# Gated FFN of a hybrid decoder step: up products by seven block products a pair, down products spread between the pairs

## The chip, the core and the metric

The kernel runs on one core of one Trainium2 chip. The metric is the time of one execution on the device in microseconds (us). TensorE is the matrix engine (PE in the profile, PEld its weight loads), VectorE is DVE, ScalarE is ACT, GpSimd is POOL, SyncE is SP. Lines L1 and so on are lines of the kernel's source.

## What is computed

One inference step of four trunk layers for 512 prompt tokens and 64 sample tokens together: 576 columns, kept as two halves of 288 (256 prompt, 32 sample). Layer 0 mixes by pools and a gated delta rule, layer 1 by a short convolution; behind each stands the channel mixer that this change is about:

```python
def conv_ffn(h, buf, w_up, conv_w, w_down):
    up = h @ w_up                                  # 1024 -> 2 * 2816
    gate, val = up[..., :D_FF], up[..., D_FF:]
    gc, new_buf = causal_dwconv(gate, buf, conv_w) # three taps
    return (jax.nn.silu(gc) * val) @ w_down, new_buf
...
        h = rmsnorm(x, norm_ffn[l])
        y, f_b = conv_ffn(h, ffn_buf[l], w_up[l], ffn_conv_w[l], w_down[l])
        x = x + y
```

The results have fp32 precision: each product is made of three, of a high part and a low part of both operands (high by high, high by low, low by high).

## The kernel before

Activations stand with features on the partitions: a row tile of 128 features by 576 tokens. A product takes a weight tile of 128 x 128 as the stationary operand and 288 token columns as the moving one; `gemm` (L216) issues, for each of the tiles of the inner dimension, six matmuls (three parts, two token halves).

Weights come as **units** of up to 1024 columns (`Feed`, L76). `load` queues a unit's transfer on SP into one of two `raw` buffers, `split` makes the two parts: ScalarE copies the high part `wh` (L111) and VectorE subtracts it for the low part `wl` (L113). `get` hands out the next unit and issues the work for those behind it. Each engine works off its instructions in the order in which they were issued; a semaphore wait on one holds up all behind it on that engine.

The channel mixer is `ffn`: the 22 tiles of hidden features go in two halves of 11. For each tile `f` (a **pair**: gate tile and value tile) come the gate product over eight k-tiles, the multiplication by the norm's factor of a token (`ext_mul`, L260 and L262), the convolution (L271, L273), silu (L1062), the value product, and the gated result `g`, split again into `gh`, `gl` (L279 to L285). After the 11 pairs of a half, eight **down products** with that half's 11 k-tiles follow, each added to its residual row tile `x` (L343). So there are 22 x 2 x 8 x 6 = 2112 matmuls for up and 8 x 22 x 6 = 1056 for down in each of the two channel mixers.

Before each channel mixer stands `out_proj`: eight products of 48 matmuls; after each, VectorE adds the residual, and `norm_operand` (L290, L291) makes high and low part of the scaled row tile, the operand of the next up products. The norm's own factor `rT` is worked out beside the first product (`norm_end`). The last down products of the second mixer and the final norm are in `last` (products at L1108, by halves of the tokens).

Of the kernel before, what the change touches and what calls it, by code (L numbers as in the profile page):

```python
# [74 lines left out]

class Feed:  # L76
    """Weights of the products in the order in which they are used: loaded ahead and split into two parts."""

    def __init__(self, tc, pool, units):
        self.tc, self.nc, self.pool, self.units = tc, tc.nc, pool, units  # L80
        self.raw, self.hl = {}, {}
        self.nd = self.ns = self.n = 0
        self.between = None
        self.slow = ()

    def cuts(self, i, w):
        """the first in halves, for an early start"""
        return ((0, 512), (512, w)) if i == 0 else ((0, w),)

    def load(self, upto):  # L90
        while self.nd < min(upto, len(self.units)):
            src, w = self.units[self.nd]
            t = self.pool.tile([128, 1024], F, tag="raw", name="raw", bufs=RAWB)
            for a, b in self.cuts(self.nd, w):
                self.nc.sync.dma_start(out=t[:, a:b], in_=src[:, a:b])
                if self.between and self.nd == 0 and a == 0:
                    self.between()
            self.raw[self.nd] = t
            self.nd += 1

    def split(self, upto):
        while self.ns < min(upto, len(self.units)):
            self.load(self.ns + 1)
            t = self.raw.pop(self.ns)
            w = self.units[self.ns][1]
            if self.ns < len(self.units) - 2:
                h, l = (self.pool.tile([128, 1024], R, tag=n, name=n, bufs=HLB) for n in ("wh", "wl"))
            else:
                h, l = (self.extra.tile([128, 768], R, tag=n, name=n, bufs=2) for n in ("eh", "el"))
            for a, b in self.cuts(self.ns, w):  # L110
                self.nc.scalar.activation(out=h[:, a:b], in_=t[:, a:b], func=AF.Copy)  # L111
                e = self.nc.gpsimd if self.ns in self.slow else self.nc.vector
                e.tensor_tensor(out=l[:, a:b], in0=t[:, a:b], in1=h[:, a:b].bitcast(F), op=SUB)  # L113
            self.hl[self.ns] = (h, l)
            self.ns += 1

    def get(self):
        i = self.n
        self.n += 1
        self.split(i + HLB)  # L120
        self.load(i + HLB + RAWB)
        return self.hl.pop(i)
# [10 lines left out]
LY = (4, 8)  # L133
# [8 lines left out]
RAWB, HLB, WB = 2, 2, 6  # L142


def body(ctx, tc, I, O):
# [9 lines left out]
    wk = pool(ctx, "wk")  # L155
    xm = pool(ctx, "xm")
    ps = pool(ctx, "ps", space=PSUM)

    cst = com.tile([128, NCST], F, name="cst")
    vec = com.tile([128, NVEC], F, name="vec")  # L160

    def C(name, rows=128):
        o, w = CST[name]
        return cst[0:rows, o:o + w]
# [9 lines left out]
    def W(name="w"):  # L174
        return wk.tile([128, 711], F, tag="w", name=name, bufs=WB)

    def bank(name="sm"):
        return ps.tile([128, 512], F, tag="sm", name=name, bufs=4)

    def acc2(name="mm"):  # L180
        return ps.tile([128, 2, 512], F, tag="mm", name=name, bufs=2)

    units = []
    for c in ORD.split():
        if c != "g":
            units.append((I["w_in_ab"][{"p": 0, "q": 4, "k": 8, "v": 12, "z": 16}[c[0]] + int(c[1])], 1024))
    for m in range(8):
        units.append((I["w_out_ab"][m], 1024))

    def ffn_units(l):  # L190
        for half in range(2):
            for f in range(half * HF, half * HF + HF):
                units.append((I["w_up"][l, f], 1024))
                units.append((I["w_up"][l, NF + f], 1024))
            for m in range(8):
                k0 = half * HF
                units.append((I["w_down"][l, m][:, k0 * 128:(k0 + 6) * 128], 768))
                units.append((I["w_down"][l, m][:, (k0 + 6) * 128:(k0 + 11) * 128], 640))

    ffn_units(0)  # L200
    for m in range(8):
        for j in (1, 2, 0):
            units.append((I["w_in_c"][j * 8 + m], 1024))
    for m in range(8):
        units.append((I["w_out_c"][m], 1024))
    ffn_units(1)
    feed = Feed(tc, wts, units)
# [3 lines left out]
    # ---------------------------------------------------------------- pieces  # L211
    def gemm(out, H, L, kmap, nks):
        """out[:, c] (+)= W.T @ x over the k-tiles of one accumulation, in the order kmap; nks: k-tiles per unit"""
        tot = sum(nks)
        oc = out if isinstance(out, list) else [out[:, 0], out[:, 1]]
        i = k0 = 0  # L216
        for nk in nks:
            h, l = feed.get()
            for _ in range(nk):
                k = kmap[i]  # L220
                kk = k - k0
                wh = h[:, kk * 128:(kk + 1) * 128]
                wl = l[:, kk * 128:(kk + 1) * 128]
                st, sp = i == 0, i == tot - 1
# [15 lines left out]
    def P2(a):  # L240
        return a.rearrange("p (c t) -> p c t", c=2)
# [1097 lines left out]
```

## Time and profile before

| | |
|---|---|
| three runs | 1388.03, 1383.38, 1387.46 us; median 1387.46 us |
| profiled execution, first to last instruction | span 1381.5 us |
| mean granted TensorE clock | 0.977 |
| TensorE busy | 98% of the span |
| VectorE, ScalarE, GpSimd busy | 55%, 36%, 13% |
| DMA | 117.37 MB, mean 85 GB/s |

The page gives the span of the profiled execution and no time of its own around it; the median of the runs stands 6.0 us above the span, the fastest run 1.9 us. The two channel mixers lie at some 318 to 731 us and 1000 to 1375 us of the span.

### The profile page before, as it was taken

The numbers are of one execution on the slowest core, as the hardware profiler recorded it, in microseconds if no ns is written. First come the engines' busy times: TensorE is split into PE (matmuls) and PEld (weight loads), VectorE is DVE, ScalarE is ACT, GpSimd is POOL, SyncE is SP. The second block draws the span as 40 slices with busy tenths as digits, with TensorE's granted clock in tenths as the row PEclk, the third lists the DMA queues.
The fourth block names the chain that finished last, engine by engine and source line by source line (L and its number), as shares of the span: only waits on it lengthen the run. The fifth ranks groups of instructions, "written<-read, shape, count | busy, mean of one in ns | idle before, by whom it ended". The sixth has DMA issues, their size and how long they took to land.

```text
span 1381.5 us, 23767 instructions
## 1 busy us (share of the span) xinstructions
PE 1348.7 (98%) x9996; PEld 1325.1 (96%) x9996; DVE 760.6 (55%) x1260; ACT 500.1 (36%) x781; POOL 174.0 (13%) x316
## 2 busy tenths in 40 slices
PE   8898999899999999999999999999999999999997
PEld 7788789899999999999999999999999999999997
DVE  7669537986555324555446454456655423555434
ACT  6463326655333212333334222234333212333333
POOL 2123112201111001111000011000111000111000
PEclk9889779999999999999999999999999999999999
DMA  5111122362222232222232222222222233222232
GB/s 200 43 40 59 40 62 76 98 191 84 77 92 74 73 85 92 92 77 82 81 84 98 80 77 92 79 85 84 77 92 79 74 84 102 77 82 88 70 84 90
DMA packets 51081, 117.37 MB, mean 85 GB/s; under 512 B 5280, under 2 KB 22048, under 8 KB 50976
## 3 DMA queue, kind: packets, MB, share of 16 engines
q1 hardware_dynamic: 50976, 115.87, 26.3%
q8 instruction: 78, 1.28, 0.4%
q14 instruction: 27, 0.22, 0.1%
HBM read 110.21 MB, written 5.64 MB: 84 GB/s over the span
## 4 chain that ended last, share of the span: by engine, by line
PE 87%; DVE 8%; ACT 3%; issue 2%; DMA 0%; SPq 0%; POOLq 0%; POOL 0%; ACTq 0%
PE mm L231 27%; PE mm L227 27%; PE mm L229 27%; DVE c L273 2%; PE mm L1108 1%; DVE Xb L690 1%; DVE tm L688 1%; PE kqs L925 1%; PE mp L731 0%; PE up L867 0%; PE kk L649 0%; ACT xwh L290 0%; ACT wh L111 0%; DMA x<-in_x_dram 0%; DVE t L311 0%
## 5 line engine op out<-in xcount | busy, mean ns | idle before, releaser
L111 ACT ACTIVATE wh<-raw 128x1024 fp32r<-128x1024 f32 (+2 forms) x211 | 206.1, 977 | 613.3 <-PE mm L229 553.1
L227 PE MATMUL mm<-xh,wh 128*128 128x288 f32 x1792 | 382.7, 295 | 0.0
L231 PE MATMUL mm<-xh,wl 128*128 128x288 f32 x1792 | 382.7, 295 | 0.0
L229 PE MATMUL mm<-xl,wh 128*128 128x288 f32 x1792 | 382.4, 295 | 0.0
L227 PEld LDWEIGHTS mm<-xh,wh 128*128 128x128 f32 x1792 | 288.0, 188 | 0.2 <-issue 0.2
L231 PEld LDWEIGHTS mm<-xh,wl 128*128 128x128 f32 x1792 | 288.0, 188 | 0.0
L229 PEld LDWEIGHTS mm<-xl,wh 128*128 128x128 f32 x1792 | 288.0, 188 | 0.0
L113 DVE TENSOR_TENSOR wl<-raw,wh 128x1024 fp32r<-128x1024 f32 (+2 forms) x193 | 214.4, 1111 | 110.1 <-ACT wh L111 105.7
L231 PE MATMUL mm<-gh,wl 128*128 128x288 f32 x788 | 169.2, 296 | 0.0
L229 PE MATMUL mm<-gl,wh 128*128 128x288 f32 x788 | 169.1, 296 | 0.0
L227 PE MATMUL mm<-gh,wh 128*128 128x288 f32 x788 | 169.1, 296 | 0.0
L227 PEld LDWEIGHTS mm<-gh,wh 128*128 128x128 f32 x788 | 127.3, 189 | 0.0
L231 PEld LDWEIGHTS mm<-gh,wl 128*128 128x128 f32 x788 | 127.3, 189 | 0.0
L229 PEld LDWEIGHTS mm<-gl,wh 128*128 128x128 f32 x788 | 127.3, 189 | 0.0
L273 DVE SCALAR_TENSOR_TENSOR c<-e,vec,c 128x592 f32<-128x592 f32 (+1 forms) x140 | 121.7, 872 | 7.7 <-ACT c L271 5.4
L260 DVE TENSOR_TENSOR e<-mm,rT 128x512 f32<-128x512 f32 x59 | 40.7, 691 | 152.9 <-PE mm L231 152.4
L266 POOL COPY nfp<-e 128x2 f32<-128x2 f32 x44 | 11.3, 257 | 629.9 <-DVE e L260 629.9
L227 PE MATMUL mm<-xwh,wh 128*128 128x288 f32 x304 | 77.5, 330 | 6.4 <-ACT wh L111 6.4
L229 PE MATMUL mm<-xwl,wh 128*128 128x288 f32 x304 | 77.3, 329 | 0.0
L231 PE MATMUL mm<-xwh,wl 128*128 128x288 f32 x304 | 77.1, 329 | 0.0
L279 DVE TENSOR_TENSOR g<-c,mm 128x512 f32<-128x512 f32 x52 | 35.8, 688 | 63.3 <-PE mm L231 63.2
L227 PEld LDWEIGHTS mm<-xwh,wh 128*128 128x128 f32 x304 | 55.5, 209 | 7.2 <-ACT wh L111 6.7
(362 smaller groups left out, 1457.6 us busy)
## 6 DMA issues: line engine op xcount, KB each, us to landing
raw<-in_w_up_dram SPq DMA_DIRECT2D x88, 512.0 KB, 3.2
raw<-in_w_down_dram SPq DMA_DIRECT2D x32, 384.0 KB, 3.1
raw<-in_w_in_c_dram SPq DMA_DIRECT2D x24, 512.0 KB, 3.2
raw<-in_w_down_dram SPq DMA_DIRECT2D x32, 320.0 KB, 2.9
raw<-in_w_in_ab_dram SPq DMA_DIRECT2D x19, 512.0 KB, 3.2
hss<-in_state_dn_dram SPq DMA_DIRECT2D x16, 256.0 KB, 3.0
raw<-in_w_out_ab_dram SPq DMA_DIRECT2D x8, 512.0 KB, 3.4
raw<-in_w_out_c_dram SPq DMA_DIRECT2D x8, 512.0 KB, 3.2
```

What stands on the lines that cost most here:

```text
L111: self.nc.scalar.activation(out=h[:, a:b], in_=t[:, a:b], func=AF.Copy)
L113: e.tensor_tensor(out=l[:, a:b], in0=t[:, a:b], in1=h[:, a:b].bitcast(F), op=SUB)
L227: PE.matmul(out=oc[c][:, 0:288], lhsT=wh, rhs=xh[:, c, :], start=st, stop=False)
L229: PE.matmul(out=oc[c][:, 0:288], lhsT=wh, rhs=xl[:, c, :], start=False, stop=False)
L231: PE.matmul(out=oc[c][:, 0:288], lhsT=wl, rhs=xh[:, c, :], start=False, stop=sp)
L260: V.tensor_tensor(out=P2(e[:, h:h + PT]), in0=a[:, :, 0:256], in1=b[:, :, 0:256], op=MUL)
L273: V.scalar_tensor_tensor(out=c[:, 0:n], in0=e[:, j:j + n], scalar=vcol(vname, idx * (h + 1) + j), in1=c[:, 0:n], op0=MUL, op1=ADD)
L279: V.tensor_tensor(out=dst[:, :, 0:256], in0=P2(c[:, 0:PT]), in1=b[:, :, 0:256], op=MUL)
L688: V.tensor_tensor(out=tv, in0=lv.to_broadcast([128, a, b]), in1=xv.to_broadcast([128, a, b]), op=MUL)
L690: V.tensor_tensor(out=uv, in0=uv, in1=tv, op=ADD)
L925: PE.matmul(out=kq[:, h * 128:(h + 1) * 128], lhsT=km[:, b].rearrange("p i t -> p (i t)"), rhs=t[:, s], start=b == 0, stop=b == 7)
L1108: PE.matmul(out=o[m][:, c, 0:288], lhsT=a[:, w], rhs=b[:, k, c], start=k == i == 0, stop=k == HF - 1 and i == 2)
```

## The change

Each pair's gate and value products are written as one product of two blocks by two blocks by two blocks: the weights' inner dimension in two halves (a and b are the gate and the value tile, each of 2 x 512 columns), the tokens in two halves. It is done in seven block products of 12 matmuls (four k-tiles, three parts) instead of eight, with sums of blocks as operands, and additions behind them. In detail:

- **Operand.** `form_operand` takes the place of `norm_operand` ahead of the channel mixers. From two row tiles (m and m + 4, hence the order `PAIR`) it makes three plain blocks (`fa`, `fb`) and four sums (`ft`), all split into two parts.
- **Weights.** `Feed` loads for each pair the full gate tile (1024 columns), a tile of two halves of 512 to which two DMAs issued from GpSimd add a third half in place (`accum_op=ADD`), and the rest of the value tile (512). VectorE makes two more sums in place, of 512 columns each (L204, L205 after). In all 3584 columns a pair are split, where 2048 were.
- **Products.** `Seven`: `head` (two block products, one of them in a bank of its own), `middle` (three), `tail` (two). Two of a pair's partial sums in PSUM are copied out by ScalarE (`sv`, L393 and L402) while the accumulation in the bank goes on; `c11`, `c22`, `c12`, `c21` of `Gated` make the four quarters of the pair's output. The sample halo and the new convolution states are copied on ScalarE instead of GpSimd.
- **Down products.** The 22 pairs go in groups of 2, 4, 4, 4, 4, 4 (`PASS`). The eight down products of a group (256 or 512 weight columns each) stand between the pairs of the next group, one ahead of a pair's tail and the others behind it; those of the last group stand at the end. So a down product has two or four k-tiles instead of 11, and each residual is added to six times instead of twice. The matmuls of the down products stay 1056.
- **Places.** `raw` has four places of 1024 and four of 512, the split weights three and three. The PSUM holds three pairs of banks and two single ones from the first channel mixer on. Tiles of the first mixer move into the places of the new operands.

```diff
+PASS = (2, 4, 4, 4, 4, 4)
+PAIR = (0, 4, 1, 5, 2, 6, 3, 7)
+def steps(tail):
+    out, f = [], 0
+    for p, n in enumerate(PASS):
+        for j in range(n):
+            out.append(("H", f))
+            if 0 < f <= PASS[0]:
+                out.append(("T", f - 1))
+            out.append(("M", f))
+            if p:
+                d = [("D", p - 1, m) for m in range(8 * j // n, 8 * (j + 1) // n)]
+                out += [*d[:1], ("T", f), *d[1:]]
+            f += 1
+    return out + [("D", len(PASS) - 1, m) for m in tail]
...
+    def sums(self, a, b):
+        self.loads.append((1024, (b[:, 512:1024], a[:, 0:512]), b[:, 0:512], 2))
...
+        if more is not None:
+            for a in (0, 512):
+                self.nc.gpsimd.dma_start(out=t[:, a:a + 512], in_=more, accum_op=ADD)
...
+            self.nc.vector.tensor_tensor(out=src[:, 0:512], in0=src[:, 0:512], in1=t[:, 0:512], op=ADD)
+            self.nc.vector.tensor_tensor(out=src[:, 512:1024], in0=src[:, 512:1024], in1=src[:, 0:512], op=ADD)
...
+    def form_operand(x, F3, m, nw, half):
+        xw = W("xw")
+        S.activation(out=P2(xw[:, 0:576]), in_=x, func=AF.Copy, scale=w)
+        if m < 4:
+            S.activation(out=fa[:, 0, j], in_=xw[:, 0:288], func=AF.Copy)
+            V.tensor_tensor(out=fa[:, 1, j], in0=xw[:, 0:288], in1=fa[:, 0, j].bitcast(F), op=SUB)
+            half[j] = xw
+            return
+        S.activation(out=fb[:, 0, j], in_=P2(xw[:, 0:576]), func=AF.Copy)
+        V.tensor_tensor(out=fb[:, 1, j], in0=P2(xw[:, 0:576]), in1=fb[:, 0, j].bitcast(F), op=SUB)
+        y = half.pop(j)
+        for i in range(2):
+            d = W("fd")
+            d1, t = d[:, 0:288], d[:, 288:576]
...
+            split_hl(ft[:, 0, j, 2 * i:2 * i + 2], ft[:, 1, j, 2 * i:2 * i + 2], P2(d[:, 0:576]))
...
+        def head(self):
+            u = feed.take()
+            yield from self.product(p, u, 0, self.x11, True, False)
+            S.activation(out=sv[:, 0:288], in_=p[:, 0:288], func=AF.Copy)
+            yield from self.product(b, u, 1, self.x21, True, True)
+            self.t.c11(sv[:, 0:288], b[:, 0:288])
+        def middle(self):
+            self.u = feed.take()
+            yield from self.product(p, self.u, 0, self.d2, False, False)
+            S.activation(out=sv[:, 288:576], in_=p[:, 0:288], func=AF.Copy)
+            u = feed.take()
+            yield from self.product(q, u, 1, self.t3, True, False)
+            yield from self.product(p, u, 0, self.d1, False, False)
+            self.t.c22(p[:, 0:288], q[:, 0:288])
+        def tail(self):
+            yield from self.product(p, self.u, 1, self.x22, False, True)
+            self.t.c12(p[:, 0:288])
+            u = feed.take()
+            yield from self.product(q, u, 0, self.t4, False, True)
+            self.t.c21(self.sv[:, 288:576], q[:, 0:288])
```

The order in which the instructions stand is not that of the source alone: the program's builder moves them. At two engines it reads so. ScalarE in a pair of the first channel mixer before (wait names: DMAHW a transfer from SP, DMASW one from GpSimd, PE, DVE and Activation the engines):

```order
L1062 ACTIVATE c<-c 128x592 [waits DVE_49]
L111 ACTIVATE wh<-raw 128x1024 [waits DMAHW4_49,PE_49,Activation_49]
L284 ACTIVATE gh<-g 128x576 [waits DVE_49]
L111 ACTIVATE wh<-raw 128x768 [waits DMAHW5_49,PE_49,Activation_49]
L271 ACTIVATE c<-e,vec 128x592 [waits DVE_49,Pool_49]
```

and in a pair of the fifth group after:

```order
L393 ACTIVATE sv<-mm 128x288 [waits PE_49,Activation_49]
L499 ACTIVATE gh<-e 128x576 [waits DVE_49]
L209 ACTIVATE wh<-raw 128x1024 [waits DMAHW6_49,PE_49,Activation_49]
L402 ACTIVATE sv<-mm 128x288 [waits PE_49]
L209 ACTIVATE wh<-raw 128x1024 [waits DVE_49,PE_49,Activation_49]
L1301 ACTIVATE v<-mm 128x288 [waits PE_49]
L209 ACTIVATE wh<-raw 128x512 [waits DMAHW3_49,PE_49]
L209 ACTIVATE wh<-raw 128x1024 [waits DMASW7_49,DMASW6_49,PE_49]
L486 ACTIVATE c<-e,vec 128x592 [waits DVE_49,Activation_49,Pool_49]
L1295 ACTIVATE nfp<-e 128x2
L1296 ACTIVATE nfs<-e 128x16
```

The splits now stand between three copies of partial sums (`sv`, `sv`, `v`), and one split (the second of 1024) waits for a sum that VectorE makes. TensorE in an up product before has two matmuls a weight part, one for each token half, in two banks:

```order
L227 MATMUL mm<-xh,wh 128x288 x2
L229 MATMUL mm<-xl,wh 128x288 x2
L231 MATMUL mm<-xh,wl 128x288 x2
L227 MATMUL mm<-xh,wh 128x288 [waits DVE_49,PE_49,Activation_49]
L227 MATMUL mm<-xh,wh 128x288
```

and after, at the end of a pair's third block product and the start of its fourth (`ft` the summed operands, `gh` and `gl` the rows of a down product):

```order
L382 MATMUL mm<-ft,wh 128x288 x2
L382 MATMUL mm<-ft,wl 128x288
L355 MATMUL mm<-gh,wh 128x288 [waits DVE_49]
L355 MATMUL mm<-gh,wh 128x288
L357 MATMUL mm<-gl,wh 128x288 x2
L382 MATMUL mm<-ft,wh 128x288 [waits Activation_49]
L382 MATMUL mm<-ft,wh 128x288
L382 MATMUL mm<-ft,wl 128x288
```

Four matmuls of a down product stand between; the fourth block product waits for ScalarE, for the second `sv` copy. VectorE of the same mixer after, from the weight sums to the third quarter:

```order
L211 TENSOR_TENSOR wl<-raw,wh 128x1024 [waits DMAHW4_49,Activation_49]
L204 TENSOR_TENSOR raw<-raw 128x512 [waits DMASW0_49,DVE_49]
L205 TENSOR_TENSOR raw<-raw 128x512 [waits DVE_49]
L211 TENSOR_TENSOR wl<-raw,wh 128x1024 [waits PE_49,Activation_49]
L1302 TENSOR_TENSOR v<-v,mm 128x288 [waits Activation_49]
L558 TENSOR_TENSOR x_88<-x_88,mm 128x576 [waits PE_49]
L211 TENSOR_TENSOR wl<-raw,wh 128x512 [waits DMAHW1_49,Activation_49]
L1282 TENSOR_TENSOR e<-mm,rT 128x256 [waits PE_49]
L1283 TENSOR_TENSOR e<-mm,rT 128x4x8
```

Before, VectorE had two 1024-wide splits and the pair's own arithmetic here; now the sum of the weights, its split and the residual of a down product stand in one queue with the quarters.

## Rows read from the trace of the kernel before

**Rows 1.** The page: busy time and share by engine; the chain that ended last.

```profile
PE 1348.7 (98%) x9996; PEld 1325.1 (96%) x9996; DVE 760.6 (55%) x1260; ACT 500.1 (36%) x781; POOL 174.0 (13%) x316
...
PE 87%; DVE 8%; ACT 3%; issue 2%; DMA 0%; SPq 0%; POOLq 0%; POOL 0%; ACTq 0%
```

**Rows 2.** Stretches of the span: busy PE, PEld, DVE, ACT, POOL (instructions), granted clock, DMA.

```profile
600.00:650.00 50.00, 50.00 (x377) 50.00 (x376) 28.51 (x40) 17.20 (x20) 8.58 (x16) 1.00 0.24 80
240.00:310.00 70.00, 66.15 (x471) 62.70 (x470) 64.75 (x152) 43.29 (x88) 10.23 (x11) 1.00 0.46 139
250.00:260.00 10.00, 8.17 (x61) 7.80 (x60) 9.94 (x33) 4.83 (x14) 3.52 (x5) 1.00 0.16 55
60.00:64.00 4.00, 1.89 (x14) 1.62 (x12) 3.10 (x18) 0.22 (x1) 0.00 (x0) 0.99 0.41 135
64.00:68.00 4.00, 4.00 (x17) 3.88 (x17) 2.31 (x11) 0.37 (x3) 0.00 (x0) 0.50 0.00 0
```

**Rows 3.** The chain in order of time, last down products: start, us, what.

```profile
1339.96 0.27 PE mm L231 x2
...
1349.56 0.27 PE mm L231 x2
1349.83 10.79 PE mm L1108 x81
```

**Rows 4.** Groups by line and form: count, busy us, mean ns, idle before.

```profile
L113 DVE TENSOR_TENSOR wl<-raw,wh 128x1024 fp32r<-128x1024 f32 x129 | 158.0, 1225 | 21.2 <-ACT wh L111 16.7 <-issue 0.2
L111 ACT ACTIVATE wh<-raw 128x1024 fp32r<-128x1024 f32 x147 | 155.7, 1059 | 418.2 <-PE mm L229 373.5 <-issue 44.3 <-PE mm L231 0.2
L273 DVE SCALAR_TENSOR_TENSOR c<-e,vec,c 128x592 f32<-128x592 f32 x104 | 86.5, 832 | 3.9 <-ACT c L271 1.8
L285 DVE TENSOR_TENSOR gl<-g,gh 128x576 fp32r<-128x576 f32 x52 | 39.1, 752 | 4.5 <-ACT gh L284 4.5
L284 ACT ACTIVATE gh<-g 128x576 fp32r<-128x576 f32 x52 | 35.7, 687 | 14.2 <-DVE g L281 7.9
L279 DVE TENSOR_TENSOR g<-c,mm 128x512 f32<-128x512 f32 x52 | 35.8, 688 | 63.3 <-PE mm L231 63.2
L1063 DVE TENSOR_TENSOR c<-c,rE 128x592 f32<-128x592 f32 x44 | 34.1, 775 | 32.5 <-ACT c L1062 32.4
L343 DVE TENSOR_TENSOR x<-x,mm 128x576 f32<-128x576 f32 x16 | 12.1, 754 | 38.5 <-PE mm L231 38.5
L291 DVE SCALAR_TENSOR_TENSOR xl<-x,vec,xh 128x576 fp32r<-128x576 f32 x12 | 9.8, 814 | 0.5
L290 ACT ACTIVATE xh<-x,vec 128x576 fp32r<-128x576 f32 x12 | 9.3, 775 | 2.7 <-DVE x L1019 1.4 <-DVE x L343 1.2
```

**Rows 5.** VectorE in a pair, in order of time: start, us, engine, line, what.

```profile
563.39 1.23 DVE L113 TENSOR_TENSOR wl<-raw,wh 128x1024 fp32r<-128x1024 f32 x1
564.53 1.70 DVE L273 SCALAR_TENSOR_TENSOR c<-e,vec,c 128x592 f32<-128x592 f32 x2
```

**Rows 6.** A down product's last two matmuls and the residual behind them.

```profile
503.67 0.43 PE L231 MATMUL mm<-gh,wl 128*128 128x288 f32 x2
...
504.13 0.75 DVE L343 TENSOR_TENSOR xr<-xr,mm 128x576 f32<-128x576 f32 x1 [2.43 <-PE mm L231]
```

**Rows 7.** Operations of 288 columns in the last norm.

```profile
1358.66 0.45 DVE L1111 TENSOR_TENSOR xr<-xr,mm 128x288 f32<-128x288 f32 x1 [2.43 <-PE mm L1108]
...
1359.15 0.45 ACT L1112 ACTIVATE sqs<-xr 128x288 f32<-128x288 f32 x1 [3.24 <-DVE xr L1111]
```

**Rows 8.** DMA issues: KB each, median us from issue to landing.

```profile
raw<-in_w_up_dram SPq DMA_DIRECT2D x88, 512.0 KB, 3.2
...
hss<-in_state_dn_dram SPq DMA_DIRECT2D x16, 256.0 KB, 3.0
```

**Rows 9.** GpSimd and VectorE side by side in the first mixer.

```profile
124.21 2.39 POOL L113 TENSOR_TENSOR wl<-raw,wh 128x1024 fp32r<-128x1024 f32 x1
124.25 2.62 DVE L690 TENSOR_TENSOR Xb<-Xb,tm 128x255 f32<-128x255 f32 x1
```

More of the change, by code (lines that the diff above doesn't have):

```diff
@@ L101, in split @@
[L101 to L115, printed above, removed]
@@ L119, in get, with ahead, take, done @@
+    def ahead(self):
+        while self.load() or self.split():
+            pass
+    def take(self):
+        self.ahead()
         self.n += 1
-        self.split(i + HLB)
-        self.load(i + HLB + RAWB)
-        return self.hl.pop(i)
+        return self.hl[self.n - 1]
+    @staticmethod
+    def done(x):
+        x[0].used(x[1])
 CY = [2, 3, 3]
@@ new lines, in gemm @@
+        h, l = u[2:]
+        for i, k in enumerate(kmap):
+            w = slice(k * 128, k * 128 + 128)
+            xh, xl = (H[k], L[k]) if isinstance(H, list) else (H[:, k], L[:, k])
+            st, sp = i == 0, i == len(kmap) - 1
+            for c in range(2):
+                PE.matmul(out=oc[c][:, 0:288], lhsT=h[:, w], rhs=xh[:, c, :], start=st, stop=False)
+            for c in range(2):
+                PE.matmul(out=oc[c][:, 0:288], lhsT=h[:, w], rhs=xl[:, c, :], start=False, stop=False)
+            for c in range(2):
+                PE.matmul(out=oc[c][:, 0:288], lhsT=l[:, w], rhs=xh[:, c, :], start=False, stop=sp)
+            if sp:
+                feed.done(u)
+            yield
@@ new lines, in ffn @@
+        nxt = None
+        tiles, g = {}, {}
+        group = [(p, j) for p, n in enumerate(PASS) for j in range(n)]
+        tail = PAIR if l == 0 else ()
+        for s in steps(tail):
+            if s[0] == "H":
+                p, j = group[s[1]]
+                if j == 0:
+                    g[p] = gtiles()
+                tiles[s[1]] = Seven(Gated(l, s[1], st, sp, ss, *g[p], j), ops_)
+                yield from tiles[s[1]].head()
+            elif s[0] == "M":
+                yield from tiles[s[1]].middle()
+            elif s[0] == "T":
+                yield from tiles[s[1]].tail()
+                if s[1] == NF - 1:
+                    nc.sync.dma_start(out=O["ffn_p"][l], in_=sp)
+                    nc.sync.dma_start(out=O["ffn_s"][l], in_=ss)
+            else:
+                end = s[1] == len(PASS) - 1
+                m = s[2]
+                if end and nxt is None:
+                    nxt = operand("xc")
+                o = acc2()
+                yield from gemm(o, *g[s[1]], range(PASS[s[1]]))
```

403 lines of the change are left out of this document (266 added, 137 removed).

## The prediction

> **What bounds the kernel now.** I read the page first: TensorE is busy for 98% of the span, and 87% of the chain that ended last is its own work [rows 1]. Then the stretches: inside a channel mixer (600 to 650 us) TensorE has no idle time at all at the full granted clock, VectorE is busy for 28.5 of 50 us and ScalarE for 17.2 [rows 2]. So in these stretches time is the number of matmuls times the time of one. That is read from the chain in order of time: from 1339.96 to 1349.56 us stand 36 steps of two matmuls, 9.60 us, or 0.1333 us each [rows 3]. A channel mixer has 3168 matmuls, 422 us, and there are two.
>
> The first mixer is another matter. From 240 to 310 us, most of it the out projection ahead of the first channel mixer, VectorE is busy for 64.75 of 70 us and TensorE idles for 3.85 [rows 2]: there VectorE is the bound, or close to it.
>
> **What is removed.** The order lists hold 9706 matmuls before and 9178 after: 528 fewer, 12 for each of 44 pairs, all of 288 columns. At 0.1333 us that is 70.4 us. Two things could spoil the price. Twelve matmuls now go one after another into one bank of PSUM, where two banks took turns; the 81 matmuls at L1108 do the same today, at 10.79 / 81 = 0.1332 us [rows 3], so nothing is lost. And the rate needs TensorE never to wait. This is where the gain can go.
>
> **A pair in the steady stretch.** From the second group on, TensorE has 84 matmuls of block products and 48 of down products a pair: 17.6 us, against 19.2 us (144) before. VectorE's work for it, by durations less the 0.09 us by which neighbours overlap (a split that lasts 1.23 us is followed after 1.14 us [rows 5]): three splits of 1024 columns, 3.42; three of 512, 1.8, and two weight sums of 512, 1.2 (0.69 us each for 512 columns); three quarters of 288, 1.1 (0.45 each [rows 7]); two multiplications by the norm factor in pieces, 0.9 (estimate from the 288 columns); two residuals, 1.33; two convolution taps, 1.7; the gate product, the value product and the low part of g, 2.1 [rows 4]. Sum 13.6 us of 17.6. ScalarE: three splits of 1.06 and three of about half, three copies of 0.45, and 2.8 for convolution, silu, g and small copies: about 9 us. Neither is the bound; what counts is the few places at which TensorE must wait for a result just asked for. The order shows three, and what stands as cover:
>
> 1. The fourth block product waits for the second `sv` copy. A hand-over from TensorE takes 0.2 us (two matmuls from 503.67 leave their slot at 503.94, the residual starts at 504.13 [rows 6]), the copy 0.45 us [rows 7]; the restart I put at 0.1 us, since no row shows one alone (bounds: 0, and 0.5, as in the second rival). Cover: four matmuls, 0.53 us. Left 0.2 us.
> 2. The sixth (x22) waits for `v` minus q. Ahead of this stand on ScalarE a 1024 split and the `v` copy, on VectorE the low part of this split: 0.07 + 1.06 + 1.14 + 0.45 + 0.1 = 2.8 us. Cover: 21 matmuls, 2.8 us. Left about nothing.
> 3. The seventh (t4) waits until the third quarter is read: 0.2 + 0.55 + 0.1 = 0.85 us, cover six matmuls, 0.8 us. Left 0.05 us.
>
> The first `sv` copy has 12 matmuls (1.6 us) for 0.75 us of work. Together 0.25 us; I take 0.35 us, since ScalarE or VectorE will now and then be found in the middle of a split. For the bounds 0.1 us, and 0.95 us if each place comes 0.2 us later. For 38 pairs (without the first three of each mixer): **+13.3 us** (3.8 to 36). Short gaps like these leave the clock alone: at 250 to 260 us TensorE was busy for 8.17 of 10 us at a granted clock of 1.00 [rows 2].
>
> **The start of each channel mixer.** Today the last row tile's operand is wanted only by the last k-tile of a product, some 5.6 us on. After the change the first two block products (24 matmuls, 3.2 us) want plain blocks, the third wants sums of the last two row tiles. The chain behind the last out product on VectorE: hand-over 0.2, residual 0.67, one 1024 split 1.14, two sums and a low part 1.4, two more sums, the low part of the first `ft`, the norm's addition and the low part of the second, about 3: 6.5 us. TensorE idles for 3.3 us, then 0.8 us for one more split in VectorE's queue. Idle time of 2.1 us at 60 to 64 us was followed by a stretch with the clock at 0.50, its lower level [rows 2]; four such us cost 2 us, I take 1.5. The first pairs have no down product as cover, and there the norm's operations join VectorE's 11 us a pair against TensorE's 11.2: 2 us. Together 7.5 us, **+15 us** for both (bounds 3.4 and 12 each).
>
> **The out projection ahead of the first.** `norm_operand` cost VectorE 0.73 us a row tile (0.81 less overlap [rows 4]); `form_operand` costs 3.9 us for two. That is 2.4 us more for each of four pairs of row tiles, 9.6 us, where VectorE has 5.25 us free in 70 [rows 2]. **+5 us** (0 to 10). The second out projection has no sample states beside it; its cover is VectorE's spare time, without which it would cost the same 9.6 us.
>
> **Group ends and the last norm.** The last group's down products want g of the last pair, some 6.8 us behind its last matmul; 17 matmuls and three down products without their last k-tile (71 matmuls, 9.5 us) cover it, and I leave 1 us each. In `last`, the half of the tokens that hides the first half's norm has 24 matmuls instead of 66; the chain to the first sum (0.2 + three of 0.45) exceeds what stands ahead of it by about 1 us. **+3 us** (0 to 9).
>
> **Moved at no cost.** Halo and state copies go from GpSimd to ScalarE, 0.6 us a pair, covered by its idle half; without that cover they cost 0.6 us a pair. The transfers: a pair now moves 1792 KB for the up products and 512 KB for the down products where it moved 1024 and some 700. SP's queue has them a pair ahead: a place for the tile to which GpSimd adds comes free when its split ends, some 15.7 us into a pair, and is wanted filled 6.2 us into the next but one, 26 us later. The plain load lands in 3.2 us; the price of an accumulating DMA no row shows. The nearest is a plain 256 KB load, 3.0 us [rows 8]: from 3.0 (taken) up to 11 each there is no wait. Ahead of it on GpSimd stands only a memset that waits for a work tile of an earlier pair.
>
> There is a rule against this part. At 124.25 us VectorE took 2.62 us for 255 columns beside a GpSimd operation of 2.39 us [rows 9], when 576 columns take 0.75 [rows 4]: one engine can shut the other out for a whole instruction. The Trainium skill, page "SBUF — State Buffer", section "SBUF: two separate sides", says more: a DMA issued from GpSimd can seem to be blocked by VectorE, as GpSimd cannot write its descriptors while VectorE uses both ports. The page's section "Who interferes with whom" excepts two-input subtractions and additions, which are nearly all that VectorE does here; no run here shows either.
>
> **The sum.** -70.4 + 13.3 + 15 + 5 + 3 = -34.1 us. The profiled span of 1381.5 us would become 1347.4 us. The median of the runs stands 6.0 us above the span and I leave that as it is: 1387.46 - 34.1 = **1353.4 us**.
>
> **Rivals.**
> - *The waits are hidden.* Pairs lose 0.1 us, starts 3.4 us, the rest nothing: 70.4 - 3.8 - 6.8 = 59.8 us gained, 1327.7 us. For it: the order puts down products just where the waits are. Against it: the chain at the start, and VectorE's 64.75 of 70 us.
> - *Each hand-over in a pair costs more* (the other side). TensorE stops at four places a pair; if its restart takes 0.5 us instead of 0.1, 1.6 us a pair go and nothing of a pair's gain is left. This is the point from which it decides: with the starts and the rest, 38 x (0.35 + 1.6) + 23 = 97 us against 70.4, or 1414 us. For it: today's mixers stop hardly ever, so no row proves a cheap restart. Half of it (0.2 to 0.3 us more) gives 1367 to 1382 us.
> - *The accumulating DMAs come late.* Two places for their tile: a pair then takes at least (3.2 + A + 9.4) / 2, with A the time of its two accumulations and 9.4 us from sum to end of split. It decides from A = 26 us, when a pair takes 19.2 us again; A = 30 gives 21.3 us, 38 x 3.4 = 128 us more than forecast, 1480 us. If VectorE's work held up the descriptors of each, they would wait for the 4 us that it is free in a pair, and A could come near it.
> - *The change does not do what it says.* The count of 528 excludes that for the matmuls.
>
> **How the numbers follow.** About 0.3%, 4 us, is what a measurement of this kernel can tell from no change. The forecast's own case, 1340 to 1366 us, 0.48; waits hidden, 1327 to 1340, 0.19; half of the dearer hand-overs, 1367 to 1382, 0.15; no change, 0.05; slower, 0.13 (hand-overs 0.08, DMAs 0.05). Faster: 0.48 + 0.19 + 0.15 = 0.82. The first three make the range: 1327 to 1382 us.
>
> **What would show it.** In the profile after: 12 matmuls fewer a pair and 0.1333 us each where TensorE runs; a steady pair of 17.8 to 18.1 us; VectorE near 13.6 us of it; a gap of about 0.2 us ahead of the fourth block product, none of note ahead of the sixth; 3 to 5 us idle at both starts with a lower clock behind it. Wrong would be: VectorE waiting for an accumulating DMA at L204, pairs over 18.5 us, or a start without a gap.

## The result, and the profile after

The changed kernel takes 1361.12 us (median of four runs, 1359.76 to 1361.99); the kernel before, measured beside it, 1387.01 us (1383.38 to 1388.03). The ratio is 0.9818, 95% interval 0.9802 to 0.9833: faster by 1.8%, 25.9 us, where 34.1 us were forecast. The profiled execution took 1361.99 us and has a span of 1360.1 us, 1.9 us less. The page of the kernel after, busy time and chain, answers to [rows 1]:

```profile
PE 1306.3 (96%) x9468; PEld 1263.8 (93%) x9468; DVE 1009.5 (74%) x1800; ACT 647.2 (48%) x1197; POOL 167.5 (12%) x272
...
PE 72%; DVE 2%; DMA 1%; ACT 1%; issue 0%; SPq 0%; DVEq 0%; ACTq 0%
...
raw<-in_w_up_dram SPq DMA_DIRECT2D x132, 256.0 KB, 3.1
...
raw<-in_w_up_dram POOLq DMA_DIRECT2D x88, 256.0 KB, 5.2
```

528 matmul records fewer, as counted, and VectorE went from 55% to 74%. The last two rows are plain and accumulating transfers of the same size: 3.1 and 5.2 us from issue to landing. Stretches of the kernel after, columns as in [rows 2]:

```profile
240.00:310.00 70.00, 66.32 (x460) 63.06 (x459) 65.58 (x158) 47.03 (x93) 10.10 (x11) 0.98 0.44 132
310.00:330.00 20.00, 12.57 (x81) 11.90 (x79) 15.12 (x25) 9.76 (x15) 2.59 (x5) 0.91 0.38 95
330.00:400.00 70.00, 66.21 (x445) 63.62 (x446) 58.57 (x103) 39.36 (x72) 10.98 (x17) 0.93 0.68 172
600.00:650.00 50.00, 50.00 (x368) 48.76 (x367) 38.52 (x64) 23.20 (x42) 4.64 (x8) 1.00 0.52 131
```

The out projection (first row) runs as before. From 310 to 400 us TensorE loses 11 us as idle time, and its granted clock is below 1. In the steady stretch (last row) TensorE looks busy all the time, but gets through 368 matmuls in 50 us, where the kernel before got through 377 [rows 2]: stops shorter than a matmul do not show as idle time. They show in the distance from pair to pair. ScalarE's first `sv` copy of the ninth and of the twenty-second pair of the first mixer, in order of time:

```profile
456.16 0.41 ACT L393 ACTIVATE sv<-mm 128x288 f32<-128x288 f32 x1 [1.08 <-PE mm L382]
...
690.17 0.41 ACT L393 ACTIVATE sv<-mm 128x288 f32<-128x288 f32 x1 [1.08 <-PE mm L382]
```

13 pairs in 234.01 us, 18.00 us each (18.03 in the second mixer), for 132 matmuls or 17.60 us. Where the 0.4 us go, TensorE in order of time at the three places of one such pair:

```profile
603.34 0.43 PE L357 MATMUL mm<-gl,wh 128*128 128x288 f32 x2
603.75 0.53 PE L382 MATMUL mm<-ft,wh 128*128 128x288 f32 x2
604.12 0.29 PE L382 MATMUL mm<-ft,wl 128*128 128x288 f32 x1
...
609.68 0.29 PE L355 MATMUL mm<-gh,wh 128*128 128x288 f32 x1
609.88 0.53 PE L382 MATMUL mm<-fb,wh 128*128 128x288 f32 x2
610.25 0.29 PE L382 MATMUL mm<-fb,wl 128*128 128x288 f32 x1
...
612.25 0.29 PE L355 MATMUL mm<-gh,wh 128*128 128x288 f32 x1
612.37 0.53 PE L382 MATMUL mm<-ft,wh 128*128 128x288 f32 x2
612.74 0.30 PE L382 MATMUL mm<-ft,wl 128*128 128x288 f32 x1
```

Two matmuls from 603.34 should hand over at 603.61; the fourth block product starts at 603.75, 0.14 us late, and its first two matmuls take 0.37 instead of 0.27 us, so the restart costs 0.10. At the sixth it is 0.07 and 0.10, at the seventh nothing and 0.10: 0.24, 0.17 and 0.09 us. Together that is 0.50 us, more than the 0.4: in a steady stretch without stops (e1 below) 132 matmuls take 17.52 us, 0.1327 us each, and measured from there a pair loses 0.48 us. What follows keeps to 0.1333 us and 0.4.

The start of the first mixer, in order of time: TensorE's last out product and where it waits, and VectorE, SP, ScalarE and GpSimd there.

```profile
317.78 0.43 PE L359 MATMUL mm<-ph,wl 128*128 128x288 f32 x2
...
319.81 0.69 DVE L204 TENSOR_TENSOR raw<-raw 128x512 f32<-128x512 f32 x1 [2.52 <-DMA raw<-in_w_up_dram]
...
321.14 0.75 DVE L1240 TENSOR_TENSOR xr<-xr,mm 128x576 f32<-128x576 f32 x1
...
322.04 0.58 PE L382 MATMUL mm<-fa,wh 128*128 128x288 f32 x1 [3.83 <-DVE xr L1240]
...
327.76 0.76 DVE L500 TENSOR_TENSOR ft<-fd,ft 128x576 fp32r<-128x576 f32 x1
...
328.60 0.33 SPq L1314 DMA_DIRECT2D sff<-in_st_ffn_dram  x1
...
328.60 1.06 ACT L209 ACTIVATE wh<-raw 128x1024 fp32r<-128x1024 f32 x1 [0.88 <-DVE ft L500]
...
328.71 0.59 POOL L1260 MEMSET rE<- 128x594 f32 x1 [10.99 <-issue]
...
330.06 0.50 PE L382 MATMUL mm<-ft,wh 128*128 128x288 f32 x2 [3.24 <-ACT sv L393]
...
342.00 0.69 DVE L204 TENSOR_TENSOR raw<-raw 128x512 f32<-128x512 f32 x1 [2.26 <-DMA raw<-in_w_up_dram]
...
344.88 0.53 PE L382 MATMUL mm<-ft,wh 128*128 128x288 f32 x2 [2.21 <-ACT wh L209]
...
346.22 0.61 PE L382 MATMUL mm<-ft,wl 128*128 128x288 f32 x1 [0.81 <-DVE wl L211]
```

VectorE waits twice for an accumulating DMA (2.52 and 2.26 us). The first time the last residual (L1240) stands behind it, and TensorE for the residual; the second time the sums of the second pair. And at 328.6 us, when the last sum of the operand is done, a load on SP, a memset on GpSimd and a split on ScalarE go off together. To measure a start I take the time from the last out product's last matmul (317.91) to the first `sv` copy of the ninth pair (456.16): 138.25 us; 882 matmuls lie between, 117.6 us. The second mixer has 128.30 us. These two numbers, the steady pair, and the time from the last pair's first copy to the end (60.2 us) are what the experiments are compared by.

### The profile page after: what moved, and what is told of

It is laid out like the page before. It is cut to its first block, busy times and chain, and to the rows that moved or that the text cites. A ratio compares the mean times of both kernels' runs of the same rounds, so it can differ in the third digit from the quotient of the medians.

```text
span 1360.1 us, 24124 instructions
## 1 busy us (share of the span) xinstructions
PE 1306.3 (96%) x9468; PEld 1263.8 (93%) x9468; DVE 1009.5 (74%) x1800; ACT 647.2 (48%) x1197; POOL 167.5 (12%) x272
## 3 DMA queue, kind: packets, MB, share of 16 engines
q0 software_dynamic: 12672, 23.07, 10.8%
## 4 chain that ended last, share of the span: by engine, by line
PE 72%; DVE 2%; DMA 1%; ACT 1%; issue 0%; SPq 0%; DVEq 0%; ACTq 0%
PE mm L382 31%; PE mm L357 12%; PE mm L355 12%; PE mm L359 12%; PE b L382 5%; DMA raw<-in_w_up_dram 1%; DVE wl L211 1%; PE rp L1422 0%; ACT wh L209 0%; DVE y L1432 0%; DVE ft L500 0%; PE sum L1384 0%; DVE fb L437 0%; ACT L1359 0%; ACT L518 0%
## 5 line engine op out<-in xcount | busy, mean ns | idle before, releaser
L209 ACT ACTIVATE wh<-raw 128x512 fp32r<-128x512 f32 (+2 forms) x333 | 286.4, 863 | 392.2 <-PE mm L357 183.7
L211 DVE TENSOR_TENSOR wl<-raw,wh 128x1024 fp32r<-128x1024 f32 (+2 forms) x315 | 303.6, 967 | 90.7 <-ACT wh L209 88.8
L382 PE MATMUL mm<-ft,wh 128*128 128x288 f32 x1408 | 295.5, 303 | 6.2 <-ACT sv L393 3.2
L382 PEld LDWEIGHTS mm<-ft,wh 128*128 128x128 f32 x1408 | 226.6, 190 | 18.0 <-ACT sv L402 8.6
L382 PE MATMUL mm<-ft,wl 128*128 128x288 f32 x704 | 210.0, 298 | 0.9 <-DVE wl L211 0.8
L184 POOL DMA_DIRECT2D raw<-in_w_up_dram x88 | 77.4, 1022 | 641.6 <-DMA raw<-in_w_up_dram 334.0
L382 PEld LDWEIGHTS mm<-ft,wl 128*128 128x128 f32 x704 | 133.8, 190 | 1.5 <-DVE wl L211 1.5
L357 PEld LDWEIGHTS mm<-gl,wh 128*128 128x128 f32 x816 | 130.2, 188 | 0.2
L355 PE MATMUL mm<-xw,wh 128*128 128x288 f32 x304 | 77.9, 331 | 6.1 <-ACT wh L209 6.1
L357 PE MATMUL mm<-xc,wh 128*128 128x288 f32 x384 | 82.4, 296 | 0.0
L355 PE MATMUL mm<-xc,wh 128*128 128x288 f32 x384 | 82.3, 296 | 0.0
L359 PE MATMUL mm<-xc,wl 128*128 128x288 f32 x384 | 82.2, 296 | 0.0
L357 PE MATMUL mm<-xw,wh 128*128 128x288 f32 x304 | 76.9, 327 | 0.0
```

Of the source, the lines that this page charges most:

```text
L184: self.nc.gpsimd.dma_start(out=t[:, a:a + 512], in_=more, accum_op=ADD)
L209: self.nc.scalar.activation(out=h[:, a:b], in_=src[:, a:b], func=AF.Copy)
L211: e.tensor_tensor(out=l[:, a:b], in0=src[:, a:b], in1=h[:, a:b].bitcast(F), op=SUB)
L355: PE.matmul(out=oc[c][:, 0:288], lhsT=h[:, w], rhs=xh[:, c, :], start=st, stop=False)
L357: PE.matmul(out=oc[c][:, 0:288], lhsT=h[:, w], rhs=xl[:, c, :], start=False, stop=False)
L359: PE.matmul(out=oc[c][:, 0:288], lhsT=l[:, w], rhs=xh[:, c, :], start=False, stop=sp)
```

## The experiments

All times are medians of four runs. The kernel before took 1385.0 us beside e1 to e4, 1387.7 us beside e5 to e8, 1386.4 us beside e9 and e10.

| | us | ratio to before | first start | second start | pair | to the end |
|---|---|---|---|---|---|---|
| the change | 1361.1 | 0.982 (0.980 to 0.983) | 138.2 | 128.3 | 18.00 | 60.2 |
| e1 | 1339.1 | 0.967 (0.964 to 0.969) | 132.5 | 124.6 | 17.52 | 60.9 |
| e2 | 1354.3 | 0.978 (0.975 to 0.980) | 129.6 | 128.2 | 18.00 | 59.9 |
| e3 | 1361.9 | 0.984 (0.981 to 0.987) | 138.2 | 130.2 | 18.00 | 60.6 |
| e4 | 1431.3 | 1.034 (1.031 to 1.036) | 152.1 | 139.1 | 19.60 | 61.9 |
| e5 | 1355.3 | 0.977 (0.976 to 0.979) | 130.7 | 128.7 | 18.01 | 60.9 |
| e6 | 1408.8 | 1.016 (1.014 to 1.018) | | | | |
| e7 | 1377.9 | 0.993 (0.992 to 0.995) | 149.7 | 133.3 | 18.00 | 60.5 |
| e8 | 1332.7 | 0.961 (0.959 to 0.963) | 126.2 | 123.7 | 17.54 | 59.5 |
| e9 | 1355.9 | 0.978 (0.975 to 0.981) | 134.4 | 127.0 | 18.02 | 59.8 |
| e10 | 1331.7 | 0.960 (0.958 to 0.963) | 128.5 | 124.8 | 17.54 | 57.2 |

**e1, two PSUM tiles.**

```diff
-            o, b = acc2(), bank("b")
-            p, q = self.p, self.q = o[:, 0], o[:, 1]
+            p, q, b = bank("p"), bank("q"), bank("b")
+            self.p, self.q = p, q
...
-    psum[:] = [pool(ctx, "ps2", space=PSUM), 2, 3]
+    psum[:] = [pool(ctx, "ps2", space=PSUM), 4, 2]
...
-            o = acc2("rp")
-            rps = [o[:, 0], o[:, 1]]
+            rps = [bank("rp"), bank("rp")]
```

> The two partial sums of a pair (p and q) get a PSUM tile each instead of the halves of one tile; the down products have two double banks instead of three, and the last norm's two factor products a bank each. Theory: the stops ahead of the fourth, sixth and seventh block product are waits for a reader of the other bank, which the program orders by the tile. Then a steady pair falls from 18.0 to 17.6 or 17.7 us, and 38 pairs give 12 to 15 us, with the last norm 1 to 2 us more: 1344 to 1349 us. Rival: what TensorE waits for is really needed and late, because ScalarE and VectorE have a queue; the pair stays at 17.9 to 18.0 us and the time within 4 us of 1361. A third outcome, slower than 1361, would be down products that wait for a residual, since they have one double bank less.

The pair falls to 17.52 us, and the time by 22 us (21 by the ratios), more than the 12 to 17 us expected: 0.48 us a pair instead of 0.3 or 0.4, and the starts gave 5.7 and 3.7 us (2.4 us of each are their five steady pairs), the last norm nothing. The order of the program shows why. TensorE in a pair of e1, only rows with a wait:

```order
L382 MATMUL p<-ft,wh 128x288 [waits Activation_49]
...
L382 MATMUL q<-ft,wh 128x288 [waits DVE_49,PE_49]
...
L382 MATMUL p<-ft,wh 128x288 [waits Activation_49]
...
L382 MATMUL p<-fb,wh 128x288 [waits Activation_49]
...
L382 MATMUL q<-ft,wh 128x288 [waits DVE_49]
```

The fourth product goes into q and has no business with the copy of p; with one tile for both it waited for it, and so did the sixth (into p) for a reader of q, and the seventh (into q) for a reader of p. In e1 the fourth follows the third at once (its wait is for a reader of an earlier pair, long done), and only the fifth waits for the copy, twelve matmuls later. The same 50 us of the steady stretch in e1:

```profile
600.00:650.00 50.00, 50.00 (x379) 50.00 (x378) 40.04 (x67) 24.10 (x44) 5.55 (x9) 1.00 0.54 138
```

379 matmuls instead of 368, and the weight loads too without a gap. The theory holds, the rival falls.

**e2, no accumulating DMAs.** The loop with `accum_op=ADD` is gone.

> The accumulating DMAs are left out (the weight sums lack one of their three halves; everything else is issued). Theory: in the steady stretch they come in time and cost nothing, so a pair stays at 18.0 us; at the start of the first mixer VectorE waits 2.5 and 2.3 us for them, and without them 3 to 6 us go: 1355 to 1358 us. Rival: they disturb the steady pairs too (ports, transfers); then a pair takes 17.6 to 17.8 us and the time falls by 10 us or more, to 1346 to 1351 us.

The theory's place was right: the pair stays at 18.00 us, the first start is 8.7 us shorter, the second the same. Its size was low (3 to 6 us). In this run no wait of VectorE for a weight transfer is left at the sums. In all 6.9 us, since the out projection ended 2 us later in the profiled execution. Not all of the 8.7 us is waiting: the 100 us from 316 us on, a row each from the changed kernel, e2 and e5:

```profile
316.00:416.00 100.00, 89.19 (x603) 85.78 (x602) 82.36 (x144) 54.04 (x97) 15.21 (x25) 0.93 0.62 156
316.00:416.00 100.00, 93.67 (x669) 90.40 (x668) 90.54 (x155) 60.10 (x108) 1.26 (x9) 0.98 0.42 133
316.00:416.00 100.00, 92.81 (x661) 89.47 (x659) 89.77 (x158) 58.48 (x107) 16.42 (x28) 0.98 0.69 172
```

In e2 TensorE is idle for 6.3 us instead of 10.8, and its granted clock is 0.98 instead of 0.93: 603 matmuls took 8.8 us more than at 0.1333 us each, and 669 take 4.5 us more here. By these rows about half of the gain is idle time that is gone (4.5 us), the other half (4.3 us) matmuls that run faster.

**e3, the first sum behind the operand.**

```diff
-        if not places.free() or max(n, more or 0) >= self.nl:
+        if not places.free() or max(n, more or 0) >= self.nl or (self.hold and more is not None):
...
+            x = self.nc.vector.tensor_tensor(out=src[:, 0:512], in0=src[:, 0:512], in1=t[:, 0:512], op=ADD)
+            if self.once:
+                self.once = False
+                self.tc.keep_in_program_order(x)
...
+    feed.hold = False
```

(`hold` ends when the out projection and its operand have been issued.)

> The first weight sum of the first mixer is kept behind the operand of the last row tile on VectorE; nothing else changes. Theory: the first gap of the mixer (3.8 us) is the last residual, which stands behind this sum while the sum waits 2.5 us for its accumulating DMA; the gap falls to about 1 us, the third block product starts 1 to 2 us earlier, and the time falls by 2 to 4 us, to 1357 to 1359 us. Rival: the sum is on the way to the third block product in any case, and the wait only moves there: within 1 us of 1361.

The theory falls: the first gap shrank from 3.83 to 0.94 us, and the start took 138.25 us again. The wait moved on: TensorE now stands 1.6 us ahead of the second block product and 3.8 us ahead of the norm's matmuls in front of the third, and VectorE's wait for the second pair's accumulating DMA grew from 2.26 to 3.6 us. That transfer landed 24.1 us behind the last out product in the changed kernel and 23.9 us here, so this wait did not depend on the sum that was moved; e5 looks for what it depends on.

**e4, the seventh product twice.**

```diff
+            yield from self.product(q, u, 0, self.t4, False, False)
             yield from self.product(q, u, 0, self.t4, False, True)
```

> The seventh block product is issued twice (twelve matmuls more a pair, the 528 that the change took away; the result counts it twice). Theory: TensorE sets the time of the pairs also after the change, and each matmul costs 0.133 us: 65 to 71 us more, 1426 to 1432 us, a steady pair of 19.5 to 19.6 us. Rival: VectorE, ScalarE or the transfers set a good part of a pair's 18.0 us; then the extra products hide in part, and it is 30 to 50 us more, 1391 to 1411 us.

70.2 us more (72 by the ratios) for 528 matmuls, and the pair 1.60 us longer for 12, 0.1333 us each: the count of matmuls has its full price, and neither VectorE, ScalarE nor the transfers bound the steady pair. TensorE's own stops stay: 144 matmuls are 19.2 us of the 19.60.

**e5, the work pool kept open.**

```diff
-    work = [pool(es, "wk"), 711, WB]
+    work = [pool(ctx, "wk"), 711, WB]
...
-    cst = work[0].tile([128, NCST - 256], F, name="cst")
+    cst = pool(es, "cs").tile([128, NCST - 256], F, name="cst")
...
-    work[:] = [gp_, 594, WX]
```

> The pool of work tiles is no longer closed ahead of the first mixer (the mixers use the same pool; a table moves to another pool to make room). Nothing else changes. Theory: the closing is a barrier: the first load of the mixer on SP's queue, the first memset on GpSimd and a split on ScalarE wait for the last sum of the operand (328.5 us), and seven weight loads, the second pair's accumulating DMAs and the first partial-sum copy stand behind them; VectorE's second wait (2.3 us) and the gaps of 3.2, 2.2 and 0.8 us come from that. Without the barrier 4 to 8 us go: 1353 to 1357 us. Rival: the start is bound by VectorE's own work on the operand and the norm; then the time stays within 2 us of 1361.

The first start is 7.6 us shorter (the whole kernel 5.8 us by the medians; the second start and the end are 0.4 and 0.7 us longer). The barrier is real: the load on SP and the memset on GpSimd that went off at 328.6 and 328.7 us start at 318.2 and 318.3 us here, 0.3 us behind the last out product (317.86). VectorE's second wait for a DMA is gone, the first (2.2 us) stays.

**e6, seven products without the interleaving.**

```diff
-            if 0 < f <= PASS[0]:
+            if j:
                 out.append(("T", f - 1))
             out.append(("M", f))
-            if p:
-                d = [("D", p - 1, m) for m in range(8 * j // n, 8 * (j + 1) // n)]
-                out += [*d[:1], ("T", f), *d[1:]]
             f += 1
+        out.append(("T", f - 1))
+        if p < len(PASS) - 1:
+            out += [("D", p, m) for m in range(8)]
```

> The seven block products stay, but the eight down products of a group stand behind its last pair, as before the change, and a pair's last two products stand behind the next pair's first two (as the first pairs of a mixer do now). Theory: the interleaved down products are what covers the hand-overs and VectorE's work; a pair then has 84 matmuls (11.2 us) against some 11 to 12 us of VectorE's work and three stops, and takes 13 to 13.5 us beside 6.4 us of down products: 1.5 to 2.2 us more a pair, 1420 to 1445 us, slower than the kernel before. Rival: the next pair's first products are cover enough, and VectorE catches up in the down products: within 15 us of 1361.

Slower than the kernel before, so the direction was right and the size too large. Four pairs and their eight down products, one period of e6:

```profile
440.00:515.40 75.40, 72.67 (x529) 70.40 (x528) 55.71 (x93) 33.50 (x60) 7.39 (x12) 1.00 0.51 126
```

528 matmuls want 70.4 us and take 75.4: 1.25 us a pair lost, where the interleaved order loses 0.4. In this order seven products are a loss, and the interleaving is worth 47 us. This kernel still has the two partial sums in one PSUM tile; with a tile each (e1, 0.48 us a pair) it might come out near the kernel before, and no run shows that.

**e7, each accumulating DMA twice.** `for a in (0, 512, 0, 512)` in place of `(0, 512)`.

> Each accumulating DMA is issued twice, one behind the other (the third half is added twice, so the weight sums are others). Theory: in the steady stretch the sums are asked for so far ahead that twice the time, some 10 us, is still hidden: a pair stays at 18.0 us; at the start of the first mixer, where VectorE waits for them, 3 to 8 us more: 1364 to 1369 us. Rival: the lead is short, or VectorE's work holds up GpSimd's descriptors, so that four a pair come late: pairs over 18.3 us, 1375 us or more.

The pair does not move, so the lead of the transfers is ample there. The starts cost 11.5 and 5.0 us more, twice what I expected, so the time lies where the rival had it, without the longer pairs that were its reason. Who waited for whom on VectorE in e7, in total (us, times, longest):

```profile
DVE raw L204 <- DMA raw<-in_w_up_dram: 14.2, 4, 5.4
```

Four waits, up to 5.4 us each; in the changed kernel there are two, 4.8 us together.

**e8, e1 and e5 and a longer cover for the last norm.**

```diff
-        for m in range(KD - 2):
+        for m in range(KD - 3):
...
-            for m in (6, 7):
+            for m in (5, 6, 7):
...
-LY = (2, 2)
+LY = (0, 2)
```

(and a bank for each half product, and a place for the squares of the third row tile.)

> Three edits together: a PSUM tile for each of the two partial sums (as in e1), the work pool kept open (as in e5), and at the end three row tiles instead of two by halves of the tokens, so that 36 matmuls instead of 24 stand beside the first half's norm. Each should show in its own stretch: steady pairs 17.5 us; the start of the first mixer 4 to 8 us shorter than in e1; the stretch from the last pair's last product to the end 1.5 to 3 us shorter. Sum 1329 to 1334 us. Rival: with the steady stops gone the start is bound by VectorE, and the last norm by its own chain; then 1337 to 1341 us, the time of e1.

1332.7 us, as expected: against e1 the first start is 6.3 us shorter, the end 1.4 us (just under the 1.5 to 3 expected). This kernel beats both: 0.961 of the time before. The start is still not free: from 310 to 410 us VectorE is busy for 93 of 100 us.

```profile
310.00:410.00 100.00, 93.48 (x683) 92.05 (x682) 92.98 (x160) 61.54 (x110) 15.50 (x26) 0.98 0.70 177
```

**e9, all four weight sums on VectorE.**

```diff
-        self.loads.append((1024, (b[:, 512:1024], a[:, 0:512]), b[:, 0:512], 2))
+        self.loads.append((1024, (b[:, 512:1024], a[:, 0:512]), None, 2))
+        self.loads.append((512, (b[:, 0:512],), None, 1))
...
-            for a in (0, 512):
-                self.nc.gpsimd.dma_start(out=t[:, a:a + 512], in_=more, accum_op=ADD)
...
+            for c in (0, 512):
+                self.nc.vector.tensor_tensor(out=t[:, c:c + 512], in0=t[:, c:c + 512], in1=m, op=ADD)
...
-RAWX, HLX, RAW1, HL1, WX = 2, 1, 4, 3, 6
+RAWX, HLX, RAW1, HL1, WX = 2, 1, 5, 3, 6
```

> The two accumulating DMAs of a pair are undone: the third half comes by a plain load into a place of its own (five places of 512 instead of four), and VectorE makes all four weight sums, two more of 0.69 us a pair. Theory: in the steady stretch VectorE has over 3 us of 18 free, so a pair stays at 18.0 to 18.2 us; the starts lose the waits for accumulating DMAs (up to 8 us, as in e2) and get 1.3 us of VectorE's work a pair, which they have no room for (2 to 4 us a mixer): 1355 to 1366 us in all. Rival: VectorE's queue is what the hand-overs hang on, and each pair gets 0.4 us or more longer: 1375 us or more, and the accumulating DMAs were worth it.

The accumulating DMAs were not worth it: without them the pair is the same, with VectorE at 85.79 of 100 us (79.39 in the changed kernel), and the starts are 3.9 and 1.3 us shorter. The waits for transfers are not gone: VectorE waits for a plain load ahead of its new sums 15 times, 7.1 us in all and 1.8 at most, and the pair does not show it.

```profile
500.00:600.00 100.00, 100.00 (x735) 97.69 (x735) 85.79 (x142) 47.12 (x87) 0.59 (x6) 1.00 0.39 121
```

**e10, e8 with the sums on VectorE.**

> The three edits of e8 with all four weight sums on VectorE (four places of 512, which now take four transfers a pair). Theory: steady pairs stay at 17.5 to 17.6 us, since TensorE waits for nothing there and VectorE gets to 15 of 17.5 us; the start of the first mixer loses the last wait for an accumulating DMA (2.1 us) with the gap of 3.4 us ahead of it, against 1.3 us a pair of more work in the first pairs: 1329 to 1334 us, no difference that can be told from e8. Rival: with so little left of VectorE's time the true waits come up, pairs of 17.8 us or more: 1342 us or more.

Not to be told from e8 (0.958 to 0.963 against 0.959 to 0.963). The starts are 2.2 and 1.1 us longer, the end is 2.3 us shorter; why the end is, no run here shows. My reading is that the sums on VectorE pay only as long as the accumulating DMAs come late for another reason, here the closed pool; e9 and e10 agree with it and do not prove it.

## Why the prediction was right, and where it was off

The forecast, 1353.4 us with 1340 to 1366 us as its own case, held. Term by term:

| term | forecast | measured | how |
|---|---|---|---|
| 528 matmuls | -70.4 | -70.4 | records; e4 puts as many back for 70.2 |
| 38 steady pairs | +13.3 | +15.8 | 19 x 0.40 + 19 x 0.43 |
| start of the first mixer | +7.5 | +18.6 | 138.25 - 117.6 - 5 x 0.4 |
| start of the second | +7.5 | +8.6 | 128.30 - 117.6 - 5 x 0.43 |
| out projection | +5 | 0, 2 us either way | its last two matmuls start at 317.78, before 318.06 |
| group ends, last norm | +3 | +4.3 | below |
| sum | -34.1 | -23.1 | |

For the last term: in the changed kernel 309 matmuls (41.2 us) lie in the last 60.0 us, 18.8 us over, 0.4 of them a pair's; before, 528 (70.4 us) in the last 84.5 us, 14.1 over. The sum lies between the difference of the two spans (-21.4) and that of the medians (-25.9). The profiled execution of before was a quick one. In the runs whose span is on record it stands 1.7 to 2.6 us below the time, so of the 6.0 us between this span and the median some 4 are this execution's own lead. In its second mixer it got through more matmuls in the same time at the same clock than in the first: pairs follow each other there by 12.48 us eight times, where 12.80 is the rule. Before, stretches of the first and of the second mixer:

```profile
340.00:440.00 100.00, 100.00 (x752) 100.00 (x752) 55.76 (x78) 32.79 (x39) 16.54 (x31) 1.00 0.26 85
980.00:1080.00 100.00, 100.00 (x772) 100.00 (x771) 57.32 (x81) 34.57 (x41) 17.25 (x32) 1.00 0.25 82
```

So it was right to add the 6.0 us, and the difference of the medians is the one to hold the sum against.

**The steady pair** came out as forecast (17.8 to 18.1 us; measured 18.0), VectorE's share too: 38.52 of 50 us, 13.9 us a pair for 13.6. The size was right and the reason half right. The three places were put at 0.2, nothing and 0.05 us, with 0.1 us for chance; they measure 0.24, 0.17 and 0.09, so the allowance for chance covered the second place, which was mis-sized. The three stops are where the order showed them, and the restart of TensorE costs the 0.1 us that I took, which settles the rival of dearer hand-overs. But I read each wait as a result that is needed. None of the three is needed as it stood: each is for a reader of the other bank, since the program orders by the PSUM tile, and e1 removes all of the 0.4 us by cutting the tile in two. A wait in the order list says what the program waits for, not that it must.

**The start of the first mixer** is the step that failed: 18.6 us for 7.5 (its upper bound was 12). By the rows from 310 to 400 us TensorE is idle for 11.2 us, where 4.1 were forecast, and its 526 matmuls are busy for 78.8 us, 8.7 us more than at 0.1333 us each, at a granted clock of 0.91 and 0.93; 1.5 us were taken for the clock and 2 us for pairs without cover. I followed the chain of the operand on VectorE and took the weights as there. Two things stood in the way. First, "moved at no cost: the transfers" took 3.0 us for an accumulating DMA and reasoned with the steady lead of 26 us; at the start there are only two places of 1024, the halves of the first sum are loaded when the out projection gives one back (312.1 us), the accumulating DMAs follow at 315.8 and 316.5 us, the first of them lands at 319.7, and VectorE waits 2.5 us. The rival of late DMAs is thus wrong for the steady pairs (e7: twice the work, no change) and right at the start (e2: 8.7 us). Second, closing the pool of work tiles makes the first load of the mixer wait for the operand's last sum, with everything behind it on SP, GpSimd and ScalarE; e5 removes that for 7.6 us. The two overlap: the second pair's accumulating DMAs are late because of the barrier. That "VectorE waits for an accumulating DMA at L204" was among the signs of a wrong forecast; it came, but twice and not in each pair.

**The out projection** cost nothing: VectorE had 65.58 busy us of 70 (64.75 before) and TensorE ran as before. So the 9.6 us of more work did not stop TensorE here, within what can be told: the last out product ends between 315.5 and 320.0 us in the executions of the changed kernel and its variants, whatever the variant. Whether part of them was only put off into the start behind it, no run separates; both terms together are 18.6 us against 12.5 forecast.

**The start of the second mixer** and the **last norm** were 1 us off each. At the second start this is partly luck: TensorE waits 6.2 us there (2.3 at most), where 4.1 were forecast, and the lower clock, for which 1.5 us were taken, did not come.

```profile
940.00:1040.00 100.00, 93.58 (x677) 90.18 (x676) 88.24 (x153) 56.42 (x103) 13.17 (x22) 1.00 0.56 136
```

This mixer has its pools open and all places from the beginning.

The rule held against the accumulating DMAs (VectorE shutting out GpSimd's descriptors) cost the steady pair nothing: e2 without them and e7 with twice as many have the pair of the changed kernel, with VectorE busy for 78 to 80 of 100 us. That agrees with the exception of the Trainium skill, page "SBUF — State Buffer", section "Who interferes with whom", for two-input sums and differences; that it is this exception, no run here shows. Nor does one show whether the transfers themselves waited for their descriptors within their 5.2 us.

Two slips in the working did not touch the sum. The down products moved 512 KB a pair before as after, not "some 700": 704 KB are the two transfers of one down product, 32 of each in the page (384 and 320 KB), 22528 KB for 44 pairs. And the range of 1367 to 1382 us for half of the dearer hand-overs belongs to a restart of 0.2 to 0.3 us, 0.1 to 0.2 us more than taken at each of four places (1369 to 1384 us); 0.2 to 0.3 us more at each would be 1384 to 1399 us.

## What to carry to other kernels

Where TensorE is the bound, matmuls saved are worth their full price, but only if something covers the new hand-overs: here the same seven products lose 1.6% or gain 1.8% by where the down products stand (both with two partial sums in one PSUM tile). Look for waits that the program makes and the data don't: two partial sums in one PSUM tile cost 0.4 to 0.5 us a pair, a pool closed at the wrong time 7.6 us at the first start. And cost a prefetch at its start as well as in its steady state: the lead that is ample in the middle (26 us by the forecast's estimate) is not there when the first places are still in use. Here idle time at such a start was paid twice: with 4.5 us less of it (e2), the matmuls behind it also lost 4.3 us less, at a granted clock of 0.98 instead of 0.93.

## What the runs showed that I had not expected

TensorE at a granted clock of 1.00 and without idle time does not always run at one rate: in the profiled execution of before 100 us held 752 matmuls of 288 columns in one stretch and 772 in another with the same instructions. By the pairs, 96 matmuls took 12.80 and 12.48 us, 0.1333 and 0.1300 us each; e1's steady pairs run at 17.52 / 132 = 0.1327. What sets it stays open. An accumulating transfer of 256 KB took 5.2 us from issue to landing where a plain one took 3.1.
